# A transformer block on one core: VectorE's passes of the late stages in the order of the program text

## The chip, the core and the metric

One Trainium2 chip, one of its cores. The metric is the device time of one execution in microseconds; lower is better. The core's engines are TensorE (PE, with its weight loads as PEld), VectorE (DVE), ScalarE (ACT), GpSimd (POOL) and SyncE (SP, which here only issues DMAs). Each of them runs its own list of instructions strictly in the order in which they stand in the built program, and waits at an instruction until the semaphores that it names are reached.

## The reference

256 tokens of width 2048 go through one residual block, in float32:

```python
h = rmsnorm(x, g_mix)
proj = h @ w_in                      # q, k, v of two mixers and two gates
merged = sigmoid(gate_sb) * (y_sb @ w_sb_out) + sigmoid(gate_ca) * (y_ca @ w_ca_out)
x = x + merged @ w_mix_out
h = rmsnorm(x, g_ffn)
g_ff, u_ff = split(h @ w_ffn_in)     # two halves of 5632 columns
x = x + (silu(g_ff) * u_ff) @ w_ffn_out
h = rmsnorm(x, g_ple)
x = x + sigmoid(h @ w_ple_gate) * (p @ w_ple_in)
return rmsnorm(x, g_final)
```

`y_sb` and `y_ca` are the outputs of the two attention mixers. The change concerns what comes behind them: the product with `w_mix_out`, the FFN, and the seam to the last product with `w_ple_gate`.

## The kernel before

**Products in three parts.** A float32 operand is written as `hi`, its value rounded to the format that TensorE reads in one pass, and `lo`, the rest. A product is then three matmuls: hi·hi, hi·lo and lo·hi (`three`, L305-307). The activations lie in tables, `T1`, `T2`, `T3`, of 16 blocks (kt) of 128 features, each with its hi and its lo. The weights come from memory raw: SP loads a tile `raw` of 128x1024, ACT casts it to `hi` (L277), DVE subtracts to get `lo` (`minus`, L257). So each weight tile needs one ACT pass and one DVE pass of 1024 columns before PE can use it, and PE spends 12 products of 512 columns on it. There are three or four buffers each of `hi` and `lo`, shared by all weights.

**Units.** Most of the work is in units (`unit`): two weight tiles side by side, 2x512 output columns, all kts. In most pairs of kts the products are done plainly; for the pairs named in an order table a Strassen-like form with seven products in place of eight is used (`split_pair`, `pair_products`). Its weights need four more DVE passes of 512 columns (`xf`, `raw`), one ACT cast (L298) and one DVE pass of 1536 columns (`T<-xf`), and its activations need sums and differences of table blocks: `sums_of` makes four DVE passes of 128 columns (`fm`), an ACT cast (L470), and a DVE pass of 512 (`FP<-fm`, `F_more<-fm`, ...). A PE sums those products in banks of their own (`su`); `mid` (L854) adds them into a tile `C`, `add_sums` (L858) adds the plain sums (`mm`).

**Between the units.** The results of a unit become the next table: PE transposes (`tp`, L482), ACT casts hi (L500, L504, L508), DVE subtracts lo (L257, L509), and `table_part` makes the forms for the pairs that need them. Before the FFN the norm's factor must reach the table: its first product runs on unscaled blocks, and once the factor is broadcast (`dg`, then the PE product `rps` at L139, then the DVE copy `p2bc` at L140) `scale_next` multiplies the blocks of T3 by it in place (L821, two passes per pair of kts) and makes the forms of T3 from them (`pair_sums`, L842).

**The order of the program.** The kernel's text describes the work piece by piece: `flush` takes a piece (two kts of one or both weight tiles), `prefetch` describes the splits of up to three pieces ahead, `products` describes the products, then the piece's post-processing, and one waiting task (a table, a norm) behind it. The FFN is 11 units of `w_ffn_in` and 6 of `w_ffn_out`, in three blocks (12, 16 and 16 kts of hidden features). What order the engines then get is not this one: the recording layer schedules the whole program and puts each engine's instructions in an order of its own choice, which keeps all dependencies. DVE is given whatever it could run first. PE's and ACT's order are chosen in the same run, in step with DVE's.

Of the kernel before, what the change touches and what calls it, by code (L numbers as in the profile page):

```python
# [52 lines left out]
def block_kernel(ctx: ExitStack, tc: tile.TileContext, x, p, w_in, w_sb_out, w_ca_out, w_mix_out,  # L53
# [100 lines left out]
    def run_task():  # L154
        name, fn = tasks.popleft()
        fn()
        if name is not None:
            done.add(name)
# [181 lines left out]
    def seed_next():  # L340

        pc = pieces[min(state["at"] + 2, len(pieces) - 1)]
        g = pc["g"]
        if g.get("seed") is not None and "ps" not in g:
            for b in range(2):
                open_sums(g)
                for t in range(2):
                    nc.scalar.copy(g["ps"][2 * b + t], g["seed"](b, t))

    def products(pc):  # L350
        g = pc["g"]
        if pc.get("pair"):
            pair_products(pc)
        elif g["kind"] == "unit":
            if pc["first"] and g["seed"] is None:
                open_sums(g)
            for i, kt in enumerate(pc["kts"]):
                a, z = pc["first"] and i == 0 and g["seed"] is None, pc["last"] and i == 1
                for t in range(2):
                    row_products(g["ps"][2 * pc["block"] + t], g["lhs"], kt, t, pc["hi"][:, i, :], pc["lo"][:, i, :], a, z)  # L360
            if g["after"] is not None and pc["block"] == 1:
                g["after"](pc["kts"])
            if pc["last"]:
                g["post"](g, pc["block"])
                state["hold"] = g["hold"] and pc["block"] == 0
        elif pc is pieces[1]:
            with tc.issue_after(state["mm"].ins):
                group_products(pc)
        else:
            group_products(pc)  # L370
        del pc["hi"], pc["lo"]
# [36 lines left out]
    def prefetch():  # L408
        while state["loaded"] < len(pieces) and state["raw"] + len(pieces[state["loaded"]]["src"]) <= RAW + state["places"]:
            load(pieces[state["loaded"]])  # L410
            state["loaded"] += 1
        room = 2 if state["at"] < 4 + KD // 2 else 4 if state["fourth"] is not None else 3
        while state["split"] < state["loaded"] and state["split"] <= state["at"] + 3:
            pc = pieces[state["split"]]
            if state["split"] > state["at"] and sum(map(size, pieces[state["at"] : state["split"] + 1])) > room:
                break
            behind = [started["p"]]
            if pc["g"] is pieces[4]["g"]:
                behind += started.get(pc["kts"][0] - 2, [])
            with ExitStack() as order:  # L420
                for i in behind:
                    order.enter_context(tc.issue_after(i.ins))
                split(pc)
            state["split"] += 1
# [11 lines left out]
    def flush(every=1, until=None, in_turn=False):  # L436

        n = 0
        while state["at"] < len(pieces) and (until is None or until not in done):
            pc = pieces[state["at"]]  # L440
            prefetch()
            products(pc)
            seed_next()
            state["at"] += 1
            n += 1
            if tasks and every and not state["hold"] and int(n / every) > int((n - 1) / every):
                if in_turn:
                    with tc.issue_after(state["mm"].ins):
                        run_task()
                else:  # L450
                    run_task()
# [737 lines left out]
        group("row", w_ple_gate[0], c * NB, range(KD), T1, ple_post(c), needs=pneed)  # L1189
    group("row", w_ple_gate[0], 3 * NB, range(KD), T1, last_post, needs=pneed, keep=keep)  # L1190
    state["ps"] = late["ps"][state["unit"] % 2 == 0]
    flush(until="ffn end")

    ple["pi"] = lp.tile([P, 2, NT, NB], F32, tag="C", name="pi")
    gf = ple["gf"] = lp.tile([P, D], F32, tag="gf", name="gf")
# [26 lines left out]
```

## Time and profile before

| | |
|---|---|
| median of 3 runs | 1456.49 us (1455.96 to 1457.09) |
| the profiled execution | 1455.66 us, of which the span from first to last instruction is 1453.9 |
| busy: PE, DVE, ACT, POOL | 1443.5, 1249.7, 829.6, 25.1 us |
| from 640 to 1400 us: PE, DVE, ACT | 760.0, 696.7, 445.7 of 760 us |
| mean granted TensorE clock | 0.998 |

From about 570 to 665 us the products with `w_mix_out` run, from there to 1365 us the FFN, then the last product and the end. Times in the views are counted from the start of the span. A row of a group of instructions gives its count, its busy time and the mean length of one; two instructions on one engine overlap a little, so the distance from one start to the next is shorter than the length. In the view of waits a row names who waited for whom, the sum, the count and the longest.

### The profile page before, as it was taken

Reading aid. Unit: us, or ns where it says so; the run is one execution under the profiler, and the core shown is the slowest. Engines: PE = TensorE matmul, PEld = TensorE weight load, DVE = VectorE, ACT = ScalarE, POOL = GpSimd, SP = SyncE. Lnnn points to the kernel's source line nnn. Section 1 sums busy time; section 2 is a strip of 40 time slices with the busy share of each in tenths; the row PEclk is TensorE's granted clock in tenths of the full one; section 3 lists DMA queues with packets and bytes.
Section 4 is the critical chain, followed back from the end, with each engine's and each line's share of the span. In section 5 each row is a group of like instructions: output and inputs, shape, how many; then the busy total and the mean of one; then the engine's idle time right before and its main releaser. Section 6 shows DMA issues by size and latency. Waiting matters only on the chain.

```text
span 1453.9 us, 18702 instructions
## 1 busy us (share of the span) xinstructions
PE 1443.5 (99%) x6837; PEld 1208.8 (83%) x6837; DVE 1249.7 (86%) x1587; ACT 829.6 (57%) x993; POOL 25.1 (2%) x44
## 2 busy tenths in 40 slices
PE   9999999999999999999999999999999999999997
PEld 7888888888888888888888888888888888888886
DVE  6979777898987767888999999999999989999785
ACT  6456555655545665555556655566655556666652
POOL 0200000000010000000000000000000000000100
PEclk9999999999999999999999999999999999999999
DMA  9866555666675655765666666666666666665871
GB/s 319 283 189 212 181 172 172 180 205 198 199 257 164 180 168 181 231 204 173 198 192 189 196 222 194 199 201 208 193 194 216 195 186 201 215 189 178 275 230 70
DMA packets 164731, 291.17 MB, mean 200 GB/s; under 512 B 9024, under 2 KB 42096, under 8 KB 164384
## 3 DMA queue, kind: packets, MB, share of 16 engines
q1 hardware_dynamic: 162528, 281.32, 62.0%
q0 software_dynamic: 2112, 8.68, 1.8%
q8 instruction: 53, 0.87, 0.2%
q14 instruction: 38, 0.31, 0.1%
HBM read 284.19 MB, written 5.77 MB: 199 GB/s over the span
## 4 chain that ended last, share of the span: by engine, by line
PE 96%; DVE 2%; DMA 1%; issue 1%; ACT 0%; DVEq 0%; SPq 0%; ACTq 0%
PE mm L307 67%; PE su L307 13%; PE mm L392 8%; PE mm L394 4%; PE tp L482 1%; DVE lo L257 1%; DMA raw<-in_w_in 1%; PE mml L307 0%; DMA raw<-in_w_ple_in 0%; PE mm L382 0%; PE xps L536 0%; DVE xf L257 0%; PE yp L709 0%; ACT hi L277 0%; PE wt L800 0%
## 5 line engine op out<-in xcount | busy, mean ns | idle before, releaser
L307 PE MATMUL mm<-hi,T 128*128 128x512 f32 x2650 | 854.6, 391 | 0.4 <-DVE v L854 0.4
L257 DVE TENSOR_TENSOR lo<-raw,hi 128x1024 fp32r<-128x1024 f32 (+1 forms) x517 | 625.1, 1221 | 121.9 <-ACT hi L277 113.0
L277 ACT CAST hi<-raw 128x1024 fp32r<-128x1024 f32 (+1 forms) x379 | 396.7, 1050 | 381.0 <-PE mm L307 257.8
L307 PEld LDWEIGHTS mm<-hi,T 128*128 128x128 f32 x2650 | 497.3, 188 | 103.0 <-issue 0.8
L307 PE MATMUL mm<-lo,T 128*128 128x512 f32 x1325 | 517.1, 391 | 0.0
L307 PEld LDWEIGHTS mm<-lo,T 128*128 128x128 f32 x1325 | 248.9, 188 | 50.7
L392 PE MATMUL mm<-T,hi 128*128 128x512 f32 x512 | 179.8, 398 | 0.0
L394 PE MATMUL mm<-T,lo 128*128 128x256 f32 x512 | 139.7, 280 | 0.0
L295 ACT CAST hi<-raw 128x1024 fp32r<-128x1024 f32 x69 | 72.7, 1053 | 76.2 <-DVE raw L257 29.5
L257 DVE TENSOR_TENSOR T<-xf,T 128x1536 fp32r<-128x1536 f32 x61 | 107.2, 1757 | 8.0 <-ACT T L298 7.2
L392 PEld LDWEIGHTS mm<-T,hi 128*128 128x128 f32 x512 | 94.6, 188 | 20.1
L257 DVE TENSOR_TENSOR xf<-raw 128x512 f32<-128x512 f32 x138 | 95.1, 689 | 13.2 <-DMA raw<-in_w_ffn_out 4.1
L394 PEld LDWEIGHTS mm<-T,lo 128*128 128x128 f32 x512 | 96.7, 189 | 2.3
L298 ACT CAST T<-xf 128x1536 fp32r<-128x1536 f32 x61 | 90.2, 1479 | 12.7 <-DVE xf L257 12.3
L292 ACT CAST hi<-raw 128x1024 fp32r<-128x1024 f32 x69 | 72.6, 1052 | 31.0 <-PE mm L307 20.5
L307 PE MATMUL mm<-T,T 128*128 128x512 f32 (+1 forms) x279 | 77.2, 371 | 0.0
L307 PE MATMUL su<-hi,T 128*128 128x512 f32 x170 | 66.1, 394 | 0.0
L307 PEld LDWEIGHTS mm<-T,T 128*128 128x128 f32 x279 | 49.3, 188 | 9.1
L854 DVE TENSOR_TENSOR C<-su,C 128x512 f32<-128x512 f32 x72 | 47.8, 686 | 0.4
L257 DVE TENSOR_TENSOR xf<-raw,xf 128x512 f32<-128x512 f32 x69 | 47.5, 689 | 0.5
L257 DVE TENSOR_TENSOR raw<-raw 128x512 f32<-128x512 f32 x69 | 47.5, 689 | 0.4
L307 PE MATMUL su<-T,FP 128*128 128x512 f32 x174 | 47.3, 389 | 0.0
(280 smaller groups left out, 1242.7 us busy)
## 6 DMA issues: line engine op xcount, KB each, us to landing
raw<-in_w_ffn_in SPq DMA_DIRECT2D x176, 512.0 KB, 4.1
raw<-in_w_in SPq DMA_DIRECT2D x160, 512.0 KB, 4.4
raw<-in_w_ffn_out SPq DMA_DIRECT2D x88, 512.0 KB, 4.4
raw<-in_w_mix_out SPq DMA_DIRECT2D x32, 512.0 KB, 4.6
raw<-in_w_ple_gate SPq DMA_DIRECT2D x32, 512.0 KB, 4.9
raw<-in_w_sb_out SPq DMA_DIRECT2D x16, 512.0 KB, 3.8
raw<-in_w_ca_out SPq DMA_DIRECT2D x16, 512.0 KB, 4.5
x<-in_x SPq DMA_DIRECT2D x4, 512.0 KB, 10.2
```

The lines of the kernel that those rows point to most:

```text
L257: return nc.vector.tensor_tensor(out, a, b, ALU.subtract)
L277: state["cast"] = nc.scalar.copy(hi[:, c : c + m], raw[:, c : c + m])
L292: nc.scalar.copy(h1, raw1)
L295: nc.scalar.copy(h2, raw2)
L298: nc.scalar.copy(xh, xf)
L307: state["mm"] = nc.tensor.matmul(ps, u, v, start=first, stop=last, skip_group_check=True)
L392: nc.tensor.matmul(ps, hi[:, i, f], lhs[:, kt, :, :].rearrange("p c s -> p (c s)"), start=a, stop=False)
L394: nc.tensor.matmul(ps[:, :S], lo[:, i, f], lhs[:, kt, 0, :], start=False, stop=z)
L482: nc.tensor.transpose(ps[:, k, t * P : (t + 1) * P], src[:, t, (k0 + k) * P : (k0 + k + 1) * P], ident)
L854: nc.vector.tensor_tensor(C[i], q, C[j], ALU.add)
```

## The change

The second `flush` behind the mixers, which describes all work from the second half of the mix product to the end of the FFN, is put under a guard that fixes DVE's order to the order of description:

```diff
     state["ps"] = late["ps"][state["unit"] % 2 == 0]
-    flush(until="ffn end")
+    with tc.manual_schedule(engines={mybir.EngineType.DVE}):
+        flush(until="ffn end")
```

No instruction is added or removed: 6792 matmuls, of which 5785 have 512 columns, and all DVE and ACT instructions are the same in number and size. DVE's list is that of the text from its 585th row on, up to the seam to the last product. PE and ACT are still ordered by the scheduler, which now has to live with DVE's fixed list, so their lists move too. SP's list is unchanged, and POOL's.

Place 1 is the first unit of the FFN, where the norm's factor arrives. DVE before, from the copy of the factor (numbers are buffer numbers; L821 scales T3, `lo` is a weight split, `af` and `fm` belong to the form of a pair):

```order
L140 COPY p2bc_91<-rps_5931 128x256
L821 TENSOR_TENSOR T3_5123<-T3_5123,p2bc_91 128x2x256 x3
L257 TENSOR_TENSOR lo_5937<-raw_5770,hi_5936 128x1024
L821 TENSOR_TENSOR T3_5123<-T3_5123,p2bc_91 128x2x256 x3
L257 TENSOR_TENSOR lo_5955<-raw_5790,hi_5954 128x1024
L821 TENSOR_TENSOR T3_5123<-T3_5123,p2bc_91 128x2x256 x2
L842 TENSOR_TENSOR af_5976<-T3_5123 128x512
L257 TENSOR_TENSOR lo_5990<-raw_5810,hi_5989 128x1024
L466 TENSOR_TENSOR fm_5978<-af_5976 128x128
L257 TENSOR_TENSOR fm_5978<-af_5976 128x128
L257 TENSOR_TENSOR lo_6008<-raw_5846,hi_6007 128x1024
```

DVE at the same place after the change, where the buffer numbers are higher by 2:

```order
L140 COPY p2bc_91<-rps_5933 128x256
L257 TENSOR_TENSOR lo_5939<-raw_5772,hi_5938 128x1024
L257 TENSOR_TENSOR lo_5957<-raw_5792,hi_5956 128x1024
L821 TENSOR_TENSOR T3_5123<-T3_5123,p2bc_91 128x2x256 x6
L842 TENSOR_TENSOR af_5978<-T3_5123 128x512
L466 TENSOR_TENSOR fm_5980<-af_5978 128x128
L257 TENSOR_TENSOR fm_5980<-af_5978 128x128
L257 TENSOR_TENSOR fm_5980<-fm_5980,af_5978 128x128
L257 TENSOR_TENSOR fm_5980<-af_5978,fm_5980 128x128
L257 TENSOR_TENSOR FP_74<-fm_5980,FP_74 128x512
L821 TENSOR_TENSOR T3_5123<-T3_5123,p2bc_91 128x2x256 x2
L257 TENSOR_TENSOR lo_5992<-raw_5812,hi_5991 128x1024
```

The split `lo_5992` (before: `lo_5990`) stood behind three L821 groups and the start of the form; now it stands behind the whole form, with its last pass, `FP<-fm`, which waits for an ACT cast. PE before, from the product that makes the factor's broadcast:

```order
L139 MATMUL rps_5931<-dg_5928,ones_80 128x256
L307 MATMUL mm0_5776<-hi_5848,T3_5123 128x512
L307 MATMUL mm0_5776<-lo_5849,T3_5123 128x512
L307 MATMUL mm0_5776<-hi_5848,T3_5123 128x512
L307 MATMUL mm1_5777<-hi_5848,T3_5123 128x512
L307 MATMUL mm1_5777<-lo_5849,T3_5123 128x512
```

PE at the same place after the change:

```order
L139 MATMUL rps_5933<-dg_5930,ones_80 128x256
L307 MATMUL mm1_5779<-hi_5914,T3_5123 128x512
L307 MATMUL mm1_5779<-lo_5915,T3_5123 128x512
L307 MATMUL mm1_5779<-hi_5914,T3_5123 128x512
L307 MATMUL mm0_5778<-hi_5956,T3_5123 128x512
L307 MATMUL mm1_5779<-hi_5956,T3_5123 128x512
L307 MATMUL mm0_5798<-lo_5939,T3_5123 128x512
```

Before, `rps` stood ahead of the three pieces 5849, 5885 and 5913, so 37 products stood between it and the first that needs a split which DVE makes after the copy (`lo_5937`). Now `rps` stands behind nearly all of them: five products stand between it and the first with `lo_5939`, 24 more between that and the first with `lo_5992`, and 24 more up to the first with `lo_6039`.

Place 2 is in the units of the FFN in which both halves of a table need a form; there are three of them. DVE before, from the first such form on (`xf`, `raw` and `lo` belong to coming weights):

```order
L466 TENSOR_TENSOR fm_6570<-af_6566 128x128
L257 TENSOR_TENSOR fm_6570<-af_6566 128x128
L257 TENSOR_TENSOR T2_72<-af_6566,T2_72 128x2x256
L257 TENSOR_TENSOR xf_6646<-raw_6496,xf_6646 128x512
L257 TENSOR_TENSOR fm_6570<-fm_6570,af_6566 128x128
L257 TENSOR_TENSOR lo_6648<-raw_6496,hi_6647 128x1024
L257 TENSOR_TENSOR lo_6650<-raw_6498,hi_6649 128x1024
L257 TENSOR_TENSOR fm_6570<-af_6566,fm_6570 128x128
L257 TENSOR_TENSOR T1_71<-xf_6646,T1_71 128x1536
L257 TENSOR_TENSOR lo_6678<-raw_6518,hi_6677 128x1024
L257 TENSOR_TENSOR T1_71<-fm_6570,T1_71 128x512
```

DVE there after the change:

```order
L466 TENSOR_TENSOR fm_6572<-af_6568 128x128
L257 TENSOR_TENSOR fm_6572<-af_6568 128x128
L257 TENSOR_TENSOR fm_6572<-fm_6572,af_6568 128x128
L257 TENSOR_TENSOR fm_6572<-af_6568,fm_6572 128x128
L257 TENSOR_TENSOR T1_71<-fm_6572,T1_71 128x512
L257 TENSOR_TENSOR T2_72<-af_6584,T2_72 128x2x256
L466 TENSOR_TENSOR fm_6588<-af_6584 128x128
L257 TENSOR_TENSOR fm_6588<-af_6584 128x128
L257 TENSOR_TENSOR fm_6588<-fm_6588,af_6584 128x128
L257 TENSOR_TENSOR fm_6588<-af_6584,fm_6588 128x128
L257 TENSOR_TENSOR T1_71<-fm_6588,T1_71 128x512
L257 TENSOR_TENSOR lo_6598<-raw_6450,hi_6597 128x1024
```

The two forms were strewn between the splits of the next weights; `lo_6596`, the counterpart of `lo_6598`, stood four rows ahead of the first of them. Now both forms stand in a block, each with its ACT cast between its fourth `fm` and its last pass, and `lo_6598` behind both. PE's list has 105 instructions, 97 products and 8 transposes, from the last `su` product that `mid` of this unit waits for to the first product with `lo_6598`.

Place 3 is the last unit of the FFN, where the table for the last product is made from `x`. DVE before (`T1<-tp` at L509 makes a lo of that table):

```order
L509 SCALAR_TENSOR_TENSOR T1_71<-tp_11174,gT_86,T1_71 128x256
L509 SCALAR_TENSOR_TENSOR T1_71<-tp_11183,gT_86,T1_71 128x256
L257 TENSOR_TENSOR raw_11091<-raw_11091,raw_11089 128x512
L257 TENSOR_TENSOR lo_11159<-raw_11022,hi_11158 128x1024
L257 TENSOR_TENSOR lo_11241<-raw_11089,hi_11240 128x1024
L257 TENSOR_TENSOR xf_11239<-raw_11091 128x512
L509 SCALAR_TENSOR_TENSOR T1_71<-tp_11174,gT_86,T1_71 128x256
```

DVE there after the change:

```order
L509 SCALAR_TENSOR_TENSOR T1_71<-tp_11194,gT_86,T1_71 128x256 x2
L509 SCALAR_TENSOR_TENSOR T1_71<-tp_11203,gT_86,T1_71 128x256 x2
L257 TENSOR_TENSOR xf_11241<-raw_11093 128x512
L257 TENSOR_TENSOR raw_11093<-raw_11093,raw_11091 128x512
L257 TENSOR_TENSOR xf_11241<-raw_11093 128x512
L257 TENSOR_TENSOR xf_11241<-raw_11091,xf_11241 128x512
L257 TENSOR_TENSOR lo_11243<-raw_11091,hi_11242 128x1024
```

`lo_11243` (before: `lo_11241`) stood between the passes of the table; now it stands behind all eight of them. On ACT, the L508 casts for `tp_11194` and `tp_11203` stand each behind the cast of a weight tile that waits for PE to give its buffer back.

## The prediction

> **What bounds the kernel now.** I read the page first, then the waits of PE, then the window that holds the changed stretch.
>
> ```profile
> span 1453.9 us, 18702 instructions
> PE 1443.5 (99%) x6837; PEld 1208.8 (83%) x6837; DVE 1249.7 (86%) x1587; ACT 829.6 (57%) x993; POOL 25.1 (2%) x44
> PE 96%; DVE 2%; DMA 1%; issue 1%; ACT 0%; DVEq 0%; SPq 0%; ACTq 0%
> ```
>
> PE is busy all the time and the chain that ended last is PE's own list. From the view of waits, PE's longest wait for DVE, and from the windows, the changed stretch and the end (columns: length, then busy time and count of PE, PEld, DVE, ACT, POOL, then the granted clock):
>
> ```profile
> PE mm L307 <- DVE v L854: 0.4, 1, 0.4
> ...
> 640.00:1400.00 760.00, 760.00 (x3422) 630.43 (x3421) 696.73 (x849) 445.66 (x498) 5.28 (x6) 1.00 0.65 202
> ...
> 1446.00:1454.00 8.00, 0.00 (x0) 0.00 (x0) 2.91 (x9) 2.21 (x3) 0.00 (x0) 0.61 0.37 131
> ```
>
> PE never waits in the 760 us. DVE is idle for 63.3 of them (8%). Why it is idle, from the waits of DVE and of ACT in that window:
>
> ```profile
> DVE lo L257 <- ACT hi L277: 38.2, 42, 1.9
> ...
> ACT hi L277 <- PE mm L307: 164.5, 95, 6.0
> ```
>
> DVE waits for casts, and these wait for PE to free a buffer: DVE is ahead. So the bound is PE's list at its own pace. That pace, from the chain in order of time (start, length, what):
>
> ```profile
> 675.42 35.38 PE mm L307 x156
> ...
> 1363.52 1.64 PE tp L482 x15
> ```
>
> A product of 512 columns costs 35.38/156 = 0.227 us, a transpose 0.109. The changed list holds the same products, so there is nothing to win in the stretch; what can change is that PE waits.
>
> **The change, part by part.** No instruction comes or goes. What the old order did was to use DVE's gaps: while a cast or a product was on its way, DVE ran another split. The new order leaves DVE standing behind each such handover, with all the splits that PE needs next queued behind it. Whether PE feels that is a matter of place: from the PE instruction that lets DVE go on, count PE's products up to the first that needs a later split, and set DVE's passes up to that split against them. The durations, first from DVE's, PE's and ACT's rows in order of time:
>
> ```profile
> 674.82 0.60 PE L139 MATMUL rps<-dg,ones 128*128 128x256 f32 x2
> 675.07 0.58 PE L307 MATMUL mm<-hi,T 128*128 128x512 f32 x1
> 675.46 0.42 DVE L140 COPY p2bc<-rps 128x256 f32<-128x256 f32 x1 [0.81 <-PE rps L139]
> 675.92 1.90 DVE L821 TENSOR_TENSOR T<-T,p2bc 128x512 fp32r<-128x512 f32 x3
> 677.73 1.22 DVE L257 TENSOR_TENSOR lo<-raw,hi 128x1024 fp32r<-128x1024 f32 x1
> ...
> 705.64 0.29 DVE L466 TENSOR_TENSOR fm<-af 128x128 f32<-128x128 f32 x1
> 705.84 0.29 DVE L257 TENSOR_TENSOR fm<-af 128x128 f32<-128x128 f32 x1
> ...
> 708.44 1.76 DVE L257 TENSOR_TENSOR T<-xf,T 128x1536 fp32r<-128x1536 f32 x1
> 710.11 0.29 DVE L257 TENSOR_TENSOR fm<-fm,af 128x128 f32<-128x128 f32 x1
> 710.31 2.36 DVE L257 TENSOR_TENSOR lo<-raw,hi 128x1024 fp32r<-128x1024 f32 x2
> 712.58 0.69 DVE L257 TENSOR_TENSOR xf<-raw 128x512 f32<-128x512 f32 x1
> ...
> 727.42 0.68 DVE L257 TENSOR_TENSOR xf<-raw 128x512 f32<-128x512 f32 x1
> 728.02 1.22 DVE L257 TENSOR_TENSOR lo<-raw,hi 128x1024 fp32r<-128x1024 f32 x1
> 729.15 0.68 DVE L257 TENSOR_TENSOR raw<-raw 128x512 f32<-128x512 f32 x1
> 729.87 0.69 DVE L257 TENSOR_TENSOR xf<-raw 128x512 f32<-128x512 f32 x1
> ...
> 731.32 1.49 ACT L298 CAST T<-xf 128x1536 fp32r<-128x1536 f32 x1 [0.27 <-DVE xf L257]
> 732.84 1.76 DVE L257 TENSOR_TENSOR T<-xf,T 128x1536 fp32r<-128x1536 f32 x1 [0.42 <-ACT T L298]
> ...
> 751.79 1.41 DVE L1059 SCALAR_TENSOR_TENSOR C<-C,r_ffn 128x512 f32<-128x512 f32 x2
> ```
>
> From start to start: 0.64 from `rps` to the copy, 0.46 to the pass behind it, 0.60 for a pass of 512 (675.92 to 677.73 for three; 727.42 to 728.02), 1.135 for a split (its result is there after 1.22), 1.67 for the pass of 1536, 0.20 for an `fm`. A pass that needs the result of the one just ahead costs 0.72 (729.15 to 729.87), since it starts when that has ended; an `fm` then 0.32. DVE takes up a cast's result 0.03 to 0.04 after its end (731.32 + 1.49 to 732.84). The other prices, from the groups of the same window:
>
> ```profile
> L509 DVE SCALAR_TENSOR_TENSOR T<-tp,gT,T 128x256 fp32r<-128x256 f32 x24 | 10.4, 483 | 0.5 <-ACT T L508 0.4
> ...
> L277 ACT CAST hi<-raw 128x1024 fp32r<-128x1024 f32 x187 | 196.2, 1053 | 198.2 <-PE mm L307 164.5 <-issue 13.8 <-PE su L307 10.1
> L298 ACT CAST T<-xf 128x1536 fp32r<-128x1536 f32 x50 | 74.0, 1480 | 10.6 <-DVE xf L257 10.1 <-PE mm L307 0.5
> L508 ACT ACTIVATE T<-tp,gT 128x256 fp32r<-128x256 f32 x24 | 10.1, 474 | 5.7 <-DVE T L509 4.1 <-PE tp L482 1.6
> L500 ACT CAST T<-af 128x512 fp32r<-128x512 f32 x11 | 6.9, 627 | 0.2
> L496 ACT COPY af<-tp 128x512 f32<-128x512 f32 x11 | 6.4, 584 | 2.2 <-PE tp L482 2.2
> L470 ACT CAST T<-fm 128x512 fp32r<-128x512 f32 x6 | 3.7, 616 | 0.2 <-DVE fm L257 0.2
> ```
>
> A form in one block is then: `af` 0.72, four `fm` until the last has ended 1.01, the cast with a handover of 0.04 on each side 0.70, and the last pass: 2.43 us from the start of `af` to the start of that pass.
>
> *Place 1, the factor's broadcast.* Time 0 is the start of `rps`. DVE copies at 0.64, starts `lo_5939` at 1.10 and has it at 2.32. PE has `rps` itself (0.25, from 674.82 to the next product at 675.07 in the timeline) and five products, to 1.38: it waits 0.94. DVE goes on: `lo_5957` to 3.37, six L821 to 6.99, `af` at 7.11, the form's last pass at 9.54, two L821 from 10.14, `lo_5992` at 11.35, there at 12.57. PE, from 2.32, has 24 products, 5.44 us, to 7.76: it waits 4.81. Then `lo_6010`, two L821 and the next form bring `lo_6039` at 19.2, against another 24 products from 12.57 to 18.01: 1.19. Sum 6.9 us. Before, 37 products (8.4 us) covered the one copy, and the forms were spread.
>
> *Place 2, two forms in one table.* Time 0 is the end of the last `su` product that `mid` waits for. DVE in order: `mid` from 0.2 (three dependent passes, one not, 2.76), two splits (2.27), four passes of `add_sums` (2.40) with a split between (1.135), two L1059 (1.41), a split, the four weight passes of a pair (2.64) and two splits: 16.3. Here ACT is late: behind 61 products (13.8) comes a weight cast that waits for a buffer, then a copy (0.58) and the cast of 1536: the pass of 1536 starts at 17.1. Then `T2<-af` at 18.8, the first form's `fm` at 19.4, its last pass at 21.1; the second `T2<-af` waits for its copy and its cast, which stand on ACT behind the first form's cast, until 22.25; then `fm`, cast and last pass to 25.15, and `lo_6598` is there at 26.4. PE has 97 x 0.227 + 8 x 0.109 = 22.9. It waits 3.5 us, in three units: 10.6 us.
>
> *Place 3, the table for the last product.* From the product that frees the buffer of the cast on ACT: cast to 1.2, L508 to 1.67, two DVE passes of 0.40; the next cast stands in front of the last L508, to 2.8, then L508 to 3.3, one pass to 3.7, four weight passes to 6.35, the split is there at 7.57. PE has 15 products, 3.4 us: 4.2 us.
>
> *Units with one form.* The same count gives DVE 20.9 us of work and about 2.5 of handovers against 23.8 of PE: nothing, with an upper bound of 1 us in each of five, and the same in the three second units of `w_ffn_out`.
>
> How a dependent pass is priced matters for a part of this. [...]
>
> The sum is 6.9 + 10.6 + 4.2 = 21.7 us. The profiled execution took 1455.66, so the same kind of execution would take 1477.4. It lies 0.83 below the median of 1456.49, and beside that median the forecast is 1478.
>
> Ends: if all handovers hide somewhere, place 1 still has 16.4 us of bare DVE work (19.2 less 0.6 for the start and 2.2 for handovers and dependences) against 12.0 of products behind `rps`, 4.4 us, and the others nothing: 1461. If each place costs a quarter to a half more (8, 15, 6) and the eight units take 1 us each, it is 37 us: 1494.
>
> **The rivals.**
>
> *PE's stock covers it; not slower.* DVE has 63 us of idle time in the window and the new handovers cost some 35. For it: the average stays under 100%. Against it: a stock is counted at a place, and at place 1 it is five products. It decides at 12.6 us of products ready at `rps`, against 6.6. Then 1456.5. That a stretch gets faster by a shorter wait elsewhere has little room: PE's idle time in it is 0, and the 8 us behind PE's last product hold the same instructions in the same order. Perhaps 1453.
>
> *Only the bare work counts* (handovers hidden, as the low end): 1461 to 1465.
>
> *PE's clock falls in the long waits.* In the last 8 us, with no product, the granted clock is 0.61 on average, so it falls within some 2 us of PE's end. Five waits of 3.5 to 4.8 us could each be followed by a stretch at half pace. The first products of the program show how long that lasts: a 128-column one takes 0.42 us up to 5.4 us (the middle one of the three lengths, in ns), and 0.27 later.
>
> ```profile
> L580 PE MATMUL warm<-ones x16: 421/421/583, 1.2 to 5.4; 128*128 128x128 f32 x16
> ...
> L482 PE MATMUL tp<-ident,C x88: 270/273/277, 710.6 to 1285.3; 128*128 128x128 f32 x88
> ```
>
> Four us at half pace lose 2, five times 10: 1488. [...]
>
> **How the numbers follow.** Places 1 to 3 as worked out: 0.58, 1470 to 1485. Clock as well: 0.17, 1483 to 1496. Bare work alone: 0.13, 1461 to 1468. No change: 0.09. Faster: 0.03. A measurement of this kernel tells about 0.2% (2.9 us) from no change. Range 1461 to 1496.
>
> **What would show it.** Right: in the new profile PE has waits for DVE splits (L307 <- `lo`) of about 20 us in all, three of them of about 1, 5 and 1 us behind `rps`, one of 3 to 4 us in each of three FFN units, one of about 4 close to the FFN's end; DVE's busy time is unchanged and DVE waits for ACT's L470 at each of the forms. Wrong: PE's waits stay under 4 us, or they lie in small pieces in all units (then DVE's pace, not the places, is the bound), or PE waits for ACT or DMA. A granted clock below 0.99 before PE's end would speak for the clock.

## The result, and the profile after

The changed kernel took 1493.36 us (median of 4 runs, 1492.6 to 1495.51), the kernel before 1456.22 us beside it (4 runs, 1455.31 to 1457.09): a ratio of 1.0258, 95% interval 1.0245 to 1.0271, or 37.1 us more. The forecast was 1478 us with a range of 1461 to 1496. So the sign was right and the time lies in the range, but 15 us behind the likeliest value.

The page of the changed kernel, its first lines, and the window of the whole stretch (length, then busy time and count of PE, PEld, DVE, ACT and POOL, then the granted clock):

```profile
span 1492.0 us, 18753 instructions
...
PE 1460.2 (98%) x6837; PEld 1212.6 (81%) x6837; DVE 1263.3 (85%) x1587; ACT 831.3 (56%) x993; POOL 24.2 (2%) x44
...
640.00:1400.00 760.00, 739.80 (x3251) 604.25 (x3251) 690.94 (x823) 427.51 (x475) 3.02 (x5) 0.99 0.61 191
```

In the same 760 us PE gets through 3251 instructions where it did 3422 before. The 171 that are missing are worth about 171 x 760/3422 = 38.0 us: nearly the whole difference of the spans (1492.0 - 1453.9 = 38.1) arises here, and about 1 us ahead of it, in the mix product. The busy share does not show its size (739.8 of 760), since part of the time is lost while PE counts as busy. The waits of PE:

```profile
PE mm L307 <- DVE lo L257: 15.3, 6, 4.5
PE su L307 <- DVE lo L257: 3.0, 5, 0.8
PE mm L307 <- ACT hi L295: 1.4, 1, 1.4
...
PE su L307 <- DVE T L509: 1.2, 2, 0.6
...
PE su L307 <- DVE T L257: 0.2, 1, 0.2
```

None of these five rows was there before. They sum to 21.1 us, 18.3 of it for weight splits, 1.4 for parts of tables and 1.4 for a cast of ACT. The rest is seen in PE's rows in order of time, here at the first of the three units with two forms:

```profile
772.02 0.84 PE L307 MATMUL su<-T,FP 128*128 128x512 f32 x3
776.13 0.50 PE L307 MATMUL mm<-lo,T 128*128 128x512 f32 x1 [3.27 <-DVE lo L257]
776.47 0.40 PE L307 MATMUL mm<-hi,T 128*128 128x512 f32 x1
...
777.67 1.06 PE L307 MATMUL mm<-hi,T 128*128 128x512 f32 x2
778.52 0.63 PE L307 MATMUL mm<-lo,T 128*128 128x512 f32 x1
...
780.65 0.55 PE L307 MATMUL mm<-lo,T 128*128 128x512 f32 x1
781.04 0.63 PE L307 MATMUL mm<-hi,T 128*128 128x512 f32 x2
```

The window of the slow products, with the granted clock behind the counts:

```profile
777.57:780.98 3.41, 3.41 (x9) 2.68 (x9) 3.31 (x5) 2.01 (x2) 0.00 (x0) 0.50 0.80 274
```

Two things beside the wait of 3.27. From 777.67 to 780.65 a product takes 0.43 us from start to start ((778.52 - 777.67)/2), not 0.227: PE runs at half its clock, 0.50, for 3.4 us. And the last product ahead of the wait starts at 772.47, the next at 776.13: 3.66 apart, 3.43 more than the pace. The view counts 0.16 less, because a product's own 0.39 us still runs, and a wait under that size does not show in it at all. So I added up, over all rows of PE, the time to the next start, less 0.227 for a product of 512 columns and 0.109 for a transpose. By stretch of the trace (the slow products, those that take about 0.43, are part of the loss):

| stretch, us | what runs | forecast | lost | of it slow products |
|---|---|---|---|---|
| 570–660 | mix product | 0 | 1.2 | 0 |
| 660–740 | first FFN unit (place 1) | 6.9 | 9.2 | 2.8 |
| 740–820, 980–1060, 1240–1320 | units with two forms (place 2) | 3 x 3.5 | 5.3, 5.2, 5.3 | 1.6, 1.2, 1.4 |
| 820–880, 1060–1150 | `w_ffn_out`, blocks 0 and 1 | 0 | 3.2, 2.2 | 0.4, 0.2 |
| 1320–1400 | seam at the FFN's end (place 3) | 4.2 | 6.2 | 1.6 |
| the rest | | 0 | 0.8 | 0.4 |
| sum | | 21.7 | 38.6 | 9.6 |

In the kernel before the same sum gives under 0.4 us in each stretch. Of the 9.6 us of slow products 8.1 lie in stretches with a granted clock of 0.50, all of them at the three places; the rest are nearly all single products beside a short wait, at full clock. On the other side stands DVE, which now stands still at handovers. Its waits from 660 to 1375 us, before and then after:

```profile
DVE T L257 <- ACT T L298: 5.7, 17, 1.5
...
DVE p2bc L140 <- PE rps L139: 0.8, 1, 0.8
...
DVE T L509 <- ACT T L508: 0.4, 2, 0.2
```

```profile
DVE T L257 <- ACT T L298: 18.1, 26, 1.6
...
DVE T L509 <- ACT T L508: 7.0, 8, 1.6
DVE F_more L257 <- ACT F_more L470: 5.2, 4, 2.8
DVE p2bc L140 <- PE rps L139: 5.1, 1, 5.1
DVE T L257 <- ACT T L470: 4.8, 6, 1.0
...
DVE F_last L257 <- ACT F_last L470: 1.8, 2, 1.0
DVE FP L257 <- ACT FP L470: 1.4, 2, 0.7
```

The handover of the forms (L470) costs DVE 5.2 + 4.8 + 1.8 + 1.4 = 13.2 us where before it cost nothing, the casts of 1536 (L298) 12.4 more, the last tables 6.6 more. It also waits for PE: 9.3 us for the `su` products ahead of `mid`, and 5.1 instead of 0.8 for `rps`, with the splits behind it.

Standing is not all. DVE's busy time is 1263.3 us where it was 1249.7, for the same 1587 passes, whose lengths add up to 1351.5 and 1352.4 us. The passes overlap less: from 660 to 1375 us 180 of them start just behind the end of the one ahead, within 0.08 us, where 51 did before. A pass that needs the one just ahead starts so (0.72 us instead of 0.60 in the rows of the kernel before), and in the text's order such passes stand next to each other.

### The profile page after: what moved, and what is told of

It is laid out like the page before. It is cut to its first block, busy times and chain, and to the rows that moved or that the text cites. A ratio compares the mean times of both kernels' runs of the same rounds, so it can differ in the third digit from the quotient of the medians.

```text
span 1492.0 us, 18753 instructions
## 1 busy us (share of the span) xinstructions
PE 1460.2 (98%) x6837; PEld 1212.6 (81%) x6837; DVE 1263.3 (85%) x1587; ACT 831.3 (56%) x993; POOL 24.2 (2%) x44
## 5 line engine op out<-in xcount | busy, mean ns | idle before, releaser
L257 DVE TENSOR_TENSOR lo<-raw,hi 128x1024 fp32r<-128x1024 f32 (+1 forms) x517 | 618.4, 1219 | 93.2 <-ACT hi L277 89.8
L277 ACT CAST hi<-raw 128x1024 fp32r<-128x1024 f32 (+1 forms) x379 | 397.8, 1052 | 314.2 <-PE mm L307 202.3
L295 ACT CAST hi<-raw 128x1024 fp32r<-128x1024 f32 x69 | 72.8, 1055 | 174.6 <-DVE raw L257 144.7
L257 DVE TENSOR_TENSOR T<-xf,T 128x1536 fp32r<-128x1536 f32 x61 | 107.1, 1756 | 19.5 <-ACT T L298 19.5
L257 DVE TENSOR_TENSOR xf<-raw 128x512 f32<-128x512 f32 x138 | 95.2, 690 | 8.7 <-DMA raw<-in_w_in 4.0
L298 ACT CAST T<-xf 128x1536 fp32r<-128x1536 f32 x61 | 90.4, 1482 | 8.8 <-DVE xf L257 8.8
L257 DVE TENSOR_TENSOR raw<-raw 128x512 f32<-128x512 f32 x69 | 47.7, 691 | 2.0
L257 DVE TENSOR_TENSOR xf<-raw,xf 128x512 f32<-128x512 f32 x69 | 47.7, 691 | 1.9
```

What stands on the lines that cost most here:

```text
L257: return nc.vector.tensor_tensor(out, a, b, ALU.subtract)
L277: state["cast"] = nc.scalar.copy(hi[:, c : c + m], raw[:, c : c + m])
L295: nc.scalar.copy(h2, raw2)
L298: nc.scalar.copy(xh, xf)
```

## The experiments

The first theory was that of the prediction: three places, at each of which a heap of passes stands ahead of the splits, with PE's clock as an extra. Rivals: DVE's pace in whole units is the bound; a fixed order is dear by itself, through ACT's and PE's lists; the slow products have nothing to do with the waits. The first four kernels ran on one chip (before: 1456.17 us), the next four on another (1456.63), e9 alone (1457.42), e10 and e11 together (1456.64). Kernels with inserted lines have other line numbers; L258 is then L257 of the text above, and so on. The edits are shown in part, with `...` for what is left out.

**e1: the order fixed from the factor's broadcast on.**

```diff
+    flush(until="p2")
     with tc.manual_schedule(engines={mybir.EngineType.DVE}):
         flush(until="ffn end")
```

> DVE's order is fixed only from the factor's broadcast on; the rows behind the broadcast stand in the same order as in the changed kernel, but the product rps is issued earlier in PE's list, with about three dozen products behind it. Theory (the wait of place 1 comes from PE's small stock at rps): the 9 us that the first FFN unit loses in the changed kernel and the 1 us in the mix unit go, the rest stays: about 1483 us (1481 to 1486), and no wait of PE over 1 us between 660 and 740 us. Rival (DVE's own list behind the broadcast, six L821 and a whole form ahead of the splits, is what PE waits for wherever rps stands): the wait of 4 to 5 us stays, 1491 us or more.

1487.09 us, ratio 1.0212 (1.0196 to 1.0227), between the two expectations. PE's waits from 660 to 740 us:

```profile
PE mm L307 <- DVE lo L257: 1.9, 2, 1.1
PE mm L307 <- ACT hi L277: 0.7, 1, 0.7
```

Half of it came true. The long wait is gone, and with it the 5.1 us for which DVE stood at `rps` (0.8 here), so the place of `rps` in PE's list made it one wait; but the stretch still loses 4.7 us (9.2 in the changed kernel), in three waits of about 1 us (1.26, 0.89 and 1.00 by the starts) and small ones. DVE is still late there, only less, and PE has more to do meanwhile.

**e2: the second form of a table later.** In the three units with two forms the second is made from the finished table five pieces (some 20 us) later; this adds one DVE pass of 512 to each.

```diff
+        put_off = len(pairs) > 2 and kt // 2 in pairs and kt // 2 - 1 in pairs and kt % 4 == 2
+        if put_off:
+            slow.append((state["at"] + 5, lambda: pair_sums(dst, kt, forms(kt))))
-        if forms is not None and kt // 2 in pairs:
+        if forms is not None and kt // 2 in pairs and not put_off:
...
```

> DVE's order is fixed as in the changed kernel, but in the three FFN units whose table needs two forms the second form is described five pieces later, made from the finished table (one DVE pass of 512 more in each, three in all). Theory (place 2 is two forms in a row ahead of the splits): in each of the three units the wait of 3.4 us and the slow products behind it, 5.3 us together, shrink to under 1 us, so 13 to 15 us are won: about 1479.5 us (1478 to 1482). Rival (DVE's pace in these units, its work against PE's, is the bound): the wait only moves to a later split or breaks into small ones, and with three more passes the time is 1493 to 1496 us.

1491.91 us, ratio 1.0243 (1.0228 to 1.0258): the theory missed by 12 us, and the rival fits. The wait of 3.4 us at 772 us is gone, but the first of these units now loses 1.42 us at 794 us and 1.78 at 817, with 1.7 in small pieces: 4.7 in all against 5.3. DVE's rows around the two forms of e2 tell why:

```profile
766.62 1.76 DVE L258 TENSOR_TENSOR T<-xf,T 128x1536 fp32r<-128x1536 f32 x1 [1.09 <-ACT T L299]
...
770.59 0.69 DVE L258 TENSOR_TENSOR T<-fm,T 128x512 fp32r<-128x512 f32 x1 [0.69 <-ACT T L473]
...
788.39 1.76 DVE L258 TENSOR_TENSOR T<-xf,T 128x1536 fp32r<-128x1536 f32 x1 [0.19 <-ACT T L299]
...
793.14 0.69 DVE L258 TENSOR_TENSOR T<-fm,T 128x512 fp32r<-128x512 f32 x1 [1.34 <-ACT T L473]
```

The second form stands alone now, and DVE stands at it all the same, even longer: 1.34 us. What DVE lost in the first heap it loses here, and PE pays 20 to 45 us later.

**e3: the waits filled.** Products with a stationary tile of zeros, added to a bank that is being summed, 14, 12, 8 and 4 of them, ahead of the piece whose split comes late.

```diff
+            for _ in range(FILL.get((g["no"], pc["kts"][0], pc["block"]), 0)):
+                nc.tensor.matmul(g["ps"][2 * pc["block"]], late["zero"], pc["hi"][:, 0, :], start=False, stop=False,
+                                 skip_group_check=True)
...
```

> The changed kernel with extra products of PE in its waits: products with a stationary tile of zeros, added to a bank that is being summed, so the sums are unchanged. 14 (3.2 us) in the wait of place 1, and 12, 8 and 4 (2.7, 1.8, 0.9 us) in those of the three units of place 2; place 3 is left as it is. DVE's list is the same. Theory (PE's clock falls behind a wait that is long enough, and the slow products of 0.43 us are that): where the idle rest is short the slow products go: none behind place 1 and the first unit of place 2, perhaps none behind the second, 5 to 8 still behind the third, where 2.5 us stay idle, and behind place 3. The waits themselves are set by DVE, so the end of each does not move; about 4 to 6 us are won: 1487.5 to 1489.5 us. Rival 1 (the slow products have another cause, such as operands that arrive late): as many of them as before, and 1493 us. Rival 2 (the extra products are not in the waits but on top of them): 1497 us or more.

1491.70 us, ratio 1.0241 (1.0226 to 1.0257): 1.7 us won, not 4 to 6, with a wide scatter (1489.2 to 1493.9). The slow products did what the theory said. PE in the first unit with two forms:

```profile
775.55 0.84 PE L307 MATMUL su<-T,FP 128*128 128x512 f32 x3
776.93 0.50 PE L307 MATMUL mm<-lo,T 128*128 128x512 f32 x1 [0.54 <-DVE lo L257]
777.26 0.40 PE L307 MATMUL mm<-hi,T 128*128 128x512 f32 x1
777.50 0.40 PE L307 MATMUL mm<-lo,T 128*128 128x512 f32 x1
777.73 0.62 PE L307 MATMUL mm<-hi,T 128*128 128x512 f32 x2
```

Full pace behind the wait. There are none behind place 1, none in the first two units, six behind the third (4 products of filling, 2.53 us lost at the wait) and eight behind place 3, left as it was. But less is won than the 5.0 us of slow products that went at place 1 and in the first two units suggest. With the filling's own time counted in (0.227 each), the first FFN unit loses 5.8 + 3.2 = 9.0 us against 9.2, the first two units of place 2 lose 1.5 + 2.7 = 4.2 and 2.2 + 1.8 = 4.0 against 5.3 and 5.2, the third 4.6 + 0.9 = 5.5 against 5.3. At place 1 nothing is won, because waits of 0.89 and 1.00 us appear further on: in the changed kernel DVE used PE's slow time to catch up. So the clock's own price is 1.1 to 1.2 us in a unit of place 2 and near nothing at place 1; if the third unit is like the other two, and with at most 1.6 at place 3, that is 3.5 to 5 us of the 37, an estimate. The four runs of e3 fit it: with a granted clock of 0.998, the value of the kernel before, one took 1489.2 us, two with 0.996 took 1491.6 and 1491.8, and one with 0.995 took 1493.9. So the run with hardly any slow products lies 4.2 us below the median of the changed kernel.

**e4: all three places mended.** The edits of e1 and e2, and the last FFN unit left to the scheduler.

```diff
-    with tc.manual_schedule(engines={mybir.EngineType.DVE}):
-        flush(until="ffn end")
+    flush(until="p2")
+    flush(until="ffn end", ordered=lambda no: no < 18)
...
```

`ordered` puts a piece under the guard when the number of its unit passes the test.

> DVE's order fixed from the factor's broadcast to the last unit but one, the second forms five pieces later, the last FFN unit left to the scheduler: all three places mended at once, with DVE's order still fixed in about 650 us of the program. Theory (the loss lies at the three places only): 3.5 us of small waits are left by a count of the instruction lists, with little slow clock: 1457 to 1462 us. Rival (a fixed order costs in all units, through ACT's handovers, and the three places are only where it shows): 1470 us or more.

1481.59 us, ratio 1.0172 (1.0155 to 1.0189). The theory of three places falls: 25 us of loss are left where it allows 1 to 6, and the rival's time came true. But the loss is not in all units: it is 4.7 us in the first FFN unit, 4.8, 4.8 and 6.3 in the units with two forms, 2.3 in the first stretch of `w_ffn_out`, 2.4 at the seam, and little elsewhere.

**The revised theory.** Here is what the prediction's average hid. Over the stretch DVE is busy 92% (696.73 of 760), but not in the units with two forms. The window of one of them, in the kernel before, the changed kernel and e5 (below):

```profile
738.00:820.00 82.00, 82.00 (x372) 67.92 (x371) 79.24 (x102) 50.76 (x58) 0.00 (x0) 1.00 0.62 197
```

```profile
738.00:820.00 82.00, 78.73 (x348) 64.80 (x347) 74.49 (x93) 47.27 (x53) 0.00 (x0) 0.98 0.59 187
```

```profile
738.00:820.00 82.00, 81.48 (x365) 66.37 (x363) 77.58 (x98) 47.86 (x55) 0.00 (x0) 1.00 0.62 191
```

Even before, DVE works 79.24 of 82 us there, 97%: it has under 3 us to spare. In like windows of the other two units, 970 to 1052 and 1220 to 1302 us, it works 78.99 and 79.10. The theory: any stand beyond that is paid by PE, at one place or another. Then moving a form does little, and filling the stand should help.

**e5: e2, with the end of a form behind the next split.** The pass that waits for ACT's cast of `fm` (L470) is described behind the next weight split, so DVE has a pass to run while ACT casts.

```diff
         nc.scalar.copy(f[:, 0], fm)
-        minus(f[:, 1], fm, f.bitcast(F32)[:, 0])
+        rest_of.append(lambda: minus(f[:, 1], fm, f.bitcast(F32)[:, 0]))
...
                 split(pc)
+            finish_forms()
...
```

> The kernel e2 (order fixed, second forms five pieces later) with one more edit: the last pass of each form of the late stages, the one that waits for ACT's cast of fm, is described behind the next weight split, so that DVE has a pass to run while ACT casts. DVE's work is that of e2. Revised theory (in the units with two forms DVE is busy 97% of PE's time even in the kernel before, so each stand of DVE behind a handover is paid by PE, wherever the form lies): with 0.7 to 1.3 us of stand less for each form, 2 to 3 us are won in each of the three units, 1 to 2 in the units with one form, 1.5 and some slow products at place 1: 1480 to 1484 us. Rival (the bare work of DVE in these units, in whatever order, is too much): within 2 us of e2, 1490 to 1493 us.

1480.21 us, ratio 1.0166 (1.0151 to 1.0181), 11.7 less than e2 with the same passes. DVE at the first form:

```profile
768.16 0.29 DVE L258 TENSOR_TENSOR fm<-af,fm 128x128 f32<-128x128 f32 x1
768.38 0.68 DVE L258 TENSOR_TENSOR T<-tp,T 128x512 fp32r<-128x512 f32 x1
768.98 1.21 DVE L258 TENSOR_TENSOR lo<-raw,hi 128x1024 fp32r<-128x1024 f32 x1
770.11 0.68 DVE L258 TENSOR_TENSOR T<-fm,T 128x512 fp32r<-128x512 f32 x1
```

No stand between the last `fm` and the form's last pass. The units with two forms lose 1.8, 1.9 and 1.9 us (4.7 each in e2), and PE does 365 instructions in the window above, where the changed kernel did 348. The rival, that DVE's bare work allows no gain, falls. From 740 to 820 us DVE's waits in the view fall from 5.0 us in e2 to 3.3, PE's loss by 2.9. That is more than the stands that were filled, so it may count too that the split now stands one pass of 0.6 us earlier in DVE's list. The edit does both at once, and no run parts them.

**e6: e5 with the order fixed from the factor's broadcast on.** The two edits of e1 and e5 together; the order stays fixed to the FFN's end.

> e5 with DVE's order fixed only from the factor's broadcast on, as in e1, and to the FFN's end as in the changed kernel. Revised theory: the 9 us of the first FFN unit and the 1 us of the mix unit go as well, and with them most of the slow products; what is left is the seam at the FFN's end (6 us) and small waits behind casts of 1536 and chained passes, 10 to 12 us: 1472 to 1477 us, and no wait of PE over 1 us before 1330 us. Rival (a fixed order is dear by itself): 1482 us or more.

1473.49 us, ratio 1.0118 (1.0101 to 1.0135): as expected. Between 570 and 1330 us no wait lost over 0.81 us, the first FFN unit loses 1.1 us, the units with two forms 1.9 to 2.0, the units of `w_ffn_out` 2.8 and 1.8, the seam 6.1. So more than half of the change's loss (37.1 to 16.9 us over the kernel before) goes although DVE's order is still fixed from the broadcast to the end of the FFN: what differs there is what the text describes behind what (e5) and the place of `rps` (e1).

**e7: the last FFN unit free**, otherwise the changed kernel (`ordered=lambda no: no < 18`).

> The changed kernel with the fixed order ending before the last FFN unit. Theory (place 3, the table for the last product, is one price of its own, 4.0 us of waits and 1.6 us of slow products): 3 to 6 us are won, 1487 to 1490 us, no wait over 0.7 us between 1340 and 1375 us. Rival (the wait there only shows a lag of DVE that it brings along from the units before): 1492 us or more.

1490.58 us, ratio 1.0234 (1.0219 to 1.0249), 34.0 us over the kernel before, where the changed kernel had 37.1. That is between the two expectations. The four waits of place 3 are gone and the stretch loses 2.8 us in small waits, not 6.2: most of place 3 is a price of its own. That the rest is a lag that comes along is not shown: in e11 below, where the units with two forms lose 1.9 us each instead of 5.1, the stretch still loses 2.5.

**e8: the order fixed only in the mix product and the first FFN unit** (`ordered=lambda no: no <= 2`).

> DVE's order fixed only in the second mix unit and the first FFN unit. Theory (each stretch pays for itself): 1.2 us in the mix unit, 9.2 us in the first FFN unit, and, since the forms and the splits of the following unit stand behind the fixed ones, one more wait of up to 3.6 us at the seam: 1466 to 1471 us, nothing lost behind 730 us. Rival (the order of PE and ACT that the scheduler chose along with a fixed DVE list is what costs, in all units): under 1462 us, or losses behind 730 us.

1469.50 us, ratio 1.0090 (1.0075 to 1.0105), as expected: 1.2 us lost in the mix product, 12.4 from 660 to 740 us. Behind that, in a row of the windows:

```profile
740.00:1400.00 660.00, 660.00 (x2968) 547.31 (x2968) 610.30 (x728) 391.52 (x434) 4.57 (x5) 1.00 0.65 202
```

PE is busy all the time again. What the order costs in a stretch is paid in it or just behind it.

**e9: PE stopped without DVE.** The kernel before, with 18 stops of PE: ACT reads the banks that are being summed into a scratch tile, and PE's next products stand behind the last read.

```diff
+            reads = IDLE.get((g["no"], pc["kts"][0], pc["block"]), 0)
+            for j in range(reads):
+                nc.scalar.copy(late["junk"], g["ps"][(2 * pc["block"] + 3 - j % 4) % 4][:, :P])
...
```

> The kernel before, its order free, with 18 stops of PE that have nothing to do with DVE: at 18 pieces of the FFN's first products ACT reads the banks that are being summed 3 to 10 times (128 columns each, into a scratch tile), and PE's next products stand behind the last read. The reads add nothing to the result. Theory (a wait of PE that is long enough lowers its clock for some us): behind stops of over about 3.3 us products at 0.43 us for 2 to 5 us, behind stops of 2.5 to 3.3 us now and then, behind stops of under 2 us none; about half a dozen such stretches in all, of 1.2 to 2.8 us of loss each. Rival (the slow products come with DVE's late splits, not with PE's idle time): none behind any stop, since DVE is ahead here. The stops themselves, some 35 to 40 us, lengthen the run to 1490 to 1500 us; with the slow products 1500 to 1510 us.

1500.31 us, one run. Five stretches of slow products, with no late split near. Two stops, which lost 2.06 and 2.24 us by the starts:

```profile
1031.00 0.84 PE L307 MATMUL mm<-T,T 128*128 128x512 f32 x3
1033.74 0.50 PE L374 MATMUL mm<-hi,T 128*128 128x512 f32 x1 [1.90 <-ACT junk L367]
1034.08 0.57 PE L377 MATMUL mm<-lo,T 128*128 128x512 f32 x1
1034.44 0.63 PE L378 MATMUL mm<-hi,T 128*128 128x512 f32 x1
...
1205.48 0.84 PE L307 MATMUL mm<-T,T 128*128 128x512 f32 x3
1208.40 0.50 PE L374 MATMUL mm<-hi,T 128*128 128x512 f32 x1 [2.08 <-ACT junk L367]
1208.73 0.40 PE L377 MATMUL mm<-lo,T 128*128 128x512 f32 x1
1208.97 0.40 PE L378 MATMUL mm<-hi,T 128*128 128x512 f32 x1
```

So idle time of PE alone brings the slow products: the rival falls. But the size that I had named was wrong. Of the eight stops that lost about 2.0 us or more five were followed by slow products, the shortest of them 2.06 us; of the nine from 0.7 to 1.6 us none was. The three without them lost 1.99, 2.24 and 2.45 us, so it is not the length of a stop alone that decides.

**e10: the edit of e5 alone**, on the changed kernel: the two forms stay in a row.

> The changed kernel with the one edit that e5 has over e2: the last pass of each form is described behind the next weight split. The two forms of a table stay in a row, as in the changed kernel. Revised theory (DVE's stands are paid, and the place of a form matters only through how much is queued behind it at that time): 0.7 us of stand less for each of the two forms of a unit and 0.7 to 1.0 in the units with one, so 1 to 1.5 us less wait in each two-form unit, 1.5 at place 1, 1 to 2 in the rest, and some of the slow products: 1483 to 1488 us. If only the stands counted and the row of two forms nothing, it would be e5's 1480; if only the row counted, 1491 us or more.

1484.12 us, ratio 1.0190 (1.0174 to 1.0205), as expected. The units with two forms lose 3.4, 4.2 and 3.1 us: less than in the changed kernel (5.3), more than with both edits (1.9). The edit of e2 is worth 0.6 us in a unit as long as the stands are there, and 1.2 to 2.3 together with the edit of e5. The reason is in DVE's list. With two forms in a row no split stands between them, so the first form's stand is not filled: it moves to the pass that waits for the second cast of `af` (L510, which is L500 of the changed kernel).

```profile
768.91 0.69 DVE L257 TENSOR_TENSOR T<-af,T 128x512 fp32r<-128x512 f32 x1 [1.82 <-ACT T L510]
```

In the changed kernel DVE stood 0.69 us at the first form's cast and 0.45 at this one.

**e11: e6 with the last FFN unit free.**

> e6 with the fixed order ending before the last FFN unit. Of e6's 17 us of loss 6 lie at the seam, and 2.5 to 3 of these stayed as small waits when e7 left the last unit free: 3 to 3.5 us are won, 1469.5 to 1471 us. Rival (the seam only shows a lag of DVE from the units before): 1473 us or more.

1469.51 us, ratio 1.0091 (1.0074 to 1.0107), as expected; the stretch of the seam loses 2.5 us. This is the best version with DVE's order fixed over nearly the whole stretch, and it does not beat the kernel before: 12.9 us are left. What they are was not tested. Two things stand there as in the changed kernel. DVE still waits 19.7 us for the casts of 1536 (5.7 in the kernel before), which no edit touched, and its busy time is still longer by 13.6 us:

```profile
PE 1452.1 (99%) x6837; PEld 1205.8 (82%) x6837; DVE 1263.3 (86%) x1590; ACT 824.7 (56%) x990; POOL 23.8 (2%) x44
```

## Why the prediction was right or wrong

*That it is slower, and by what.* Right. PE waits for DVE's splits, and DVE waits at handovers. e5 and e10 edit only what is described behind what for DVE, and their loss against the kernel before is 23.6 and 27.5 us, not 37.1. PE's and ACT's lists move too, but little: compared by names without buffer numbers, e10 has 39 of PE's 6837 instructions and 9 of ACT's 993 in another place than the changed kernel. At place 1 PE's list does bear on it, by the place of `rps`. Two signs of the forecast failed: DVE's busy time was not unchanged but 13.6 us longer, and close to the FFN's end there was no wait of about 4 us but four smaller ones.

*Place 1.* Forecast: 0.94, 4.81 and 1.19 of waits. Measured: 0.66 and 4.65 by the starts, the third not in the changed kernel, where PE was slow just then; e3, with PE at full pace, shows 0.89 and 1.00. e1 confirms the role of the few products between `rps` and the splits. The term was too small by about 2 us: the count ended with the third split, and e3 shows a wait of 1.00 us behind it.

*Place 2.* Forecast 3.5 us in three units; the waits lost 3.43, 3.45 and 3.43. The sum was right but its reading was not: e2 removed the heap at the place, and the loss came back 20 to 45 us later. The step that failed is the count from one PE instruction up to one split, as if what follows started afresh. With DVE at 96 to 97% in these units it does not.

*Place 3.* Forecast 4.2 in one wait for a split; the four waits lost 4.0 by the starts. The sum was right, its shape was not: only the last, 0.95, is for the split. PE stood already at parts of the table (0.74 and 0.78, L509) and at a cast of ACT (1.54, L295), which the count passed over because it looked only at the split behind them.

*Units with one form at nothing, with at most 1 us in each of eight.* The forecast took the lower end, and this step failed. The `w_ffn_out` stretches lost 3.2 and 2.2 and the rest 0.8, three quarters of the bound, and the mix product, which the sum does not name, 1.2: a term mis-sized by about 7 us, and the largest error. DVE has little to spare there as well: in the kernel before it works 77.91 of the 82 us from 820 on (95%), where the average is 92%.

*The clock.* It stood among the rivals, at 0.17 and 10 us, as an alternative to the waits of the three places. It came in addition, behind all five long waits (the four of 3.4 to 4.7 us and the group at place 3), with 8.1 us of slow products; but e3 speaks for only some 3.5 to 5 us of them as a loss on top, as part of PE's slow time covers waits that come otherwise. So the 37 us are, by estimate, 21.7 as worked out, some 7 in the other units, about 4 for the clock, and the rest at places 1 and 2, which in e3, with its filling counted in, lose 9.0 and 4.0 to 4.2 us, not 6.9 and 3.5. That 1493.36 lies in the range is in part luck. Its upper end was worked out from dearer places and 1 us in each of eight units; the units came near that, the places did only in part, and the clock, which that sum leaves out, filled the rest.

*PE's stock covers it, or only bare work counts.* Both wrong: there are 21.1 us of waits in the view, and e5 wins back 11.7 us with the same passes. But the work is not the same in every order either: 13.6 us of DVE's overlap are gone.

*A dependent pass* at 0.72 us, against 0.60, holds: in the changed kernel the four weight passes of a pair start at 760.57, 761.30, 762.03 and 762.75 us, 0.72 to 0.73 apart, and the split behind them 0.61 later. The forecast had two such steps there, and there are three. What the forecast missed is how many there are: its sums for the three places hold twelve, by the author's count. Over the whole stretch, by the count above, 129 more passes start just behind the one ahead, which at 0.12 each is about 15 us, an estimate of the size of the 13.6 by which DVE's busy time grew. How much of that reaches PE no run shows.

## What to carry to other kernels

Take an engine's spare time from the stage, not from the whole run: 92% over 760 us was 97% where it mattered, and there the stands of the engine at its handovers came out as waits of its consumer, though one form was moved by 20 us. When an engine runs in a fixed order, describe a pass that waits for another engine behind one that does not: one edit of this kind (e5 against e2) won 11.7 us. Look at busy time for the same passes too: here it grew by 13.6 us, with 180 passes just behind the one ahead where 51 were. And do not add slow-clock time to waits as if they were independent: time that a slow consumer needs was, at place 1, time in which its late producer caught up (9.2 us lost with 2.8 of slow products, 9.0 with none).

## What the runs showed of the hardware

The slow stretches lie on a regular grid in time. In the trace of the changed kernel the granted clock is 0.50 from 695.65 to 702.47, 777.57 to 780.98, 1016.50 to 1019.91, 1275.91 to 1279.32 and 1368.07 to 1371.48 us: four stretches of 3.41 us, and one of twice that at place 1, where the wait itself reaches 0.88 us into it. Their ends are 78.51, 238.93, 259.41 and 92.16 us apart, and divided by 23, 70, 76 and 27 each of these gives 3.413. A window is one step of this grid in what follows. With the grid taken in each run from the edges of its granted clock, a stop of 2.06 us that lay in one window (e9, the first rows above) brought half the clock, and one of 3.44 us in e1 did not (granted clock 1.00 from 980 to 1060 us); it lay with 1.74 us in one window and 1.70 in the next:

```profile
1008.24 0.84 PE L307 MATMUL su<-T,FP 128*128 128x512 f32 x3
1012.36 0.50 PE L307 MATMUL mm<-lo,T 128*128 128x512 f32 x1 [3.28 <-DVE lo L257]
1012.70 0.40 PE L307 MATMUL mm<-hi,T 128*128 128x512 f32 x1
```

What goes with the fall in these runs is the time lost within one window, all waits in it added up. In the changed kernel, between 570 and 1400 us, five windows at full clock lost 2.09 to 3.41 us, and behind each of them the granted clock is 0.50; no other lost more than 1.68, and behind none of those did it fall. The wait at 772 us, 3.43 by the starts, lies across an edge at 774.15: the clock stays at 1.00 behind the window with its first 1.45 us and falls behind the one with the other 1.98, which lost 2.09 in all. Over all 13 kernels, in the same stretch, there are 29 windows at full clock in which PE lost 2.07 us or more, each with 0.50 behind it, and none with 2.05 us or less that has it. The second stop in the rows of e9 is one with 2.05: of its 2.24 us the rest lay in the next window. A window at half clock was followed by another where PE lost 1.1 us or more in it, its slow products left out (five times, place 1 of the changed kernel among them), and by full clock where it lost 0.83 or less. Place 3 fits that too: no single wait there lost more than 1.54 us, but the last two fell into one window, from 1364.66 us on, which lost 2.6. These figures are read off the traces and were not tested by a kernel of their own.
